# Left-side sums of an FFN computed once, kept in DRAM and fetched back; second part's down with four pairs by seven products

## The chip, the cores and the metric

One core of one Trainium2 chip. The time is device microseconds of one launch, the median of the runs given; lower is better. The core's engines that matter here are TensorE (PE in the profile, with PEld for its weight loads), VectorE (DVE), ScalarE (ACT), GpSimd (POOL) and SyncE (SP), which issues DMAs. Each engine works through its own instructions in a fixed order and waits on semaphores for the others.

## The reference

One decoder block on 256 tokens of width 2048, in f32:

```python
h = h + 0.5 * swiglu(rms_norm(h), w_gu1, w_down1)
h = h + hybrid_mixer(rms_norm(h), w_in, ..., w_out)
h = h + 0.5 * swiglu(rms_norm(h), w_gu2, w_down2)
h = h + sigmoid(rms_norm(h) @ w_pg) * (p @ w_pp)
out = rms_norm(h)
```

`swiglu(x)` is `(silu(x @ gate) * (x @ up)) @ w_down` with an inner width of 5632. The change touches the two FFNs only.

## The kernel before, in words

**Products in f32.** Every f32 weight tile `raw` is split into a rounded part `whi` (cast on ACT, L74) and a rest `wlo` (subtraction on DVE, L75); the left operand is split in the same way (`nTh` and `nTl`, or `hTh` and `hTl` for down). A product is three matmuls of 512 columns: whi by hi, wlo by hi, whi by lo. A *plain pair* is one `raw` tile of 512 KB (two k tiles by 512 columns) and 12 matmuls: two k tiles, two halves of the tokens, three each. `raw` has four buffers and is loaded on SP's queue; `whi` and `wlo` have three each.

**Seven products for eight.** A part of each large product is done by a scheme of Strassen's kind. Blocks of weights come as four quarters `R` (loads on POOL's queue, L276, but on SP's for the first such group of an FFN). Seven sums of them are made one after another, partly in DMA (L311) and partly on DVE (L304), and each is split into `shi` (ACT, L295) and `slo` (DVE, L296), which have two buffers each. Each of the seven products (`product`, L334 to L336) takes 3 matmuls for each of `ns` pairs. After the third and the fourth, result banks are added to each other over a copy `part` (ACT, L341; DVE, L342). Four of the seven need sums on the left side: `halves` adds hi and lo into `S` (L452), makes four differences in place (L458), and splits the result into `Sh` (ACT, L460) and `Sl` (DVE, L461), for two pairs at a time.

**Groups.** The inner width comes in eleven blocks of 512, in three parts: blocks 0 to 2, 3 to 6 and 7 to 10. A part is a list of gate-up groups (`gu`, one for each block, banks g and u) and then two down groups (`dn`, banks d, two blocks of 512 output columns each). `plan` writes the order of the weights by hand: through the plain pairs of a group it spreads the seven products of the *following* group, one behind each plain pair from the second or third on, and the loads of the quarters for the group after that. The tile framework then schedules all instructions into one order for each engine, which the change can alter even where the source does not. Lanes of generators are advanced by one step behind each plain pair (`lanes.step()`): lane 0 carries `down_input` (gated result, transposed by way of DRAM, to `hTh` and `hTl`), lane 1 carries `halves`.

**Around the change.** `halves("gu")` is called at the start of an FFN and again in the second down group of parts one and two, three times in all with the same input, since `Sh` and `Sl` have one buffer that down's sums also use. `halves("dn")` is called in the last gate-up group of each part. `NS_DOWN` was (2, 3, 3). For a third single pair `halves` yields once more, takes `S` from tag "nat" (four buffers) instead of "sil" (one), and keeps the sum in program order. `down_input` of a part's last block yields `last` times ahead of its last step: 3 for parts of four blocks, else 2.

Of the kernel before, what the change touches and what calls it, by code (L numbers as in the profile page):

```python
# [26 lines left out]
PARTS = ((0, 3), (3, 7), (7, 11))  # L27


NS = 4  # L30
NS_DOWN = tuple(3 if i1 - i0 == 4 else 2 for i0, i1 in PARTS)


W_IN_ORDER = (2, 0, 4, 3, 1, 5, 8, 10, 12, 9, 11, 13, 6, 7)
# [9 lines left out]
def block_kernel(ctx, tc, a, out):  # L44
    nc = tc.nc
# [14 lines left out]
    lanes = Lanes(4)  # L60
    dr = ctx.enter_context(tc.tile_pool(name="dr", bufs=1, space=bass.MemoryType.DRAM))
# [181 lines left out]
    current, sides = [None], {}  # L243
# [107 lines left out]
    def plan(n):  # L351
# [8 lines left out]
        groups = []  # L360
        for p, (i0, i1) in enumerate(PARTS):
            for i in range(i0, i1):
                plain = PLAIN[n]
                if i < plain:
                    src = [([a[f"w_gu{n}0"][2 * i + b][g] for g in range(KD // 2)], None) for b in range(2)]
                else:
                    src = [sources("w_gu" + n, 2 * (i - plain) + b) for b in range(2)]
                groups.append(Group("gu", p, [x[0] for x in src], [x[1] for x in src], NS if i >= plain else 0,
                                    len(groups) % 2))
            for nb in (0, 2):  # L370
                src = [sources(f"w_down{n}{p}", nb + b) for b in range(2)]
                groups.append(Group("dn", p, [x[0] for x in src], [x[1] for x in src], NS_DOWN[p], len(groups) % 2, nb))
        if n == "2":
            src = [sources("w_behind", b) for b in range(2)]
            groups.append(Group("behind", len(PARTS), [x[0] for x in src], [x[1] for x in src], NS_BEHIND,
# [41 lines left out]
    order += [("pair", a["w_pg"][2][g]) for g in range(KD // 2)] + [("pair", a["w_pp"][2])]  # L417
    order.append(("pair", a["w_pp"][3]))

    def halves(kind, his, los, ns, wait=0):  # L420


        for _ in range(wait):
            yield
        fp = current[0]

        sh = fp.tile([P, NS, 2, 2, P], F32R, tag="Sh", name="Sh")
        sl = fp.tile([P, NS, 2, 2, P], F32R, tag="Sl", name="Sl")

        def side(i, g):  # L430
            if i in (0, 4, 6):
                k, t = 2 * (g % 2) + (i > 0), i // 6
                c = slice(t * P, (t + 1) * P)
                return his[g // 2][:, k, c], los[g // 2][:, k, c]
            j, t = {1: (1, 1), 2: (0, 0), 3: (0, 1), 5: (1, 0)}[i]
            return sh[:, g, j, t, :], sl[:, g, j, t, :]

        sides[kind] = side

        for g0 in range(0, ns, 2):  # L440
            n = min(2, ns - g0)
            hi, lo = his[g0 // 2], los[g0 // 2]
            keep = lambda ins: ins
            if g0 and n == 1:

                keep = tc.keep_in_program_order
                yield
            if n == 2:
                x = fp.tile([P, 2 * NB], F32, tag="sil", name="S")
            else:  # L450
                x = act.tile([P, NB], F32, tag="nat", name="S", bufs=4)
            keep(nc.vector.tensor_tensor(out=x, in0=hi[:, 0:2 * n].bitcast(F32).rearrange("p k x -> p (k x)"),  # L452
                                         in1=lo[:, 0:2 * n].bitcast(F32).rearrange("p k x -> p (k x)"), op=ALU.add))
            xv = x.rearrange("p (g j t y) -> p g j t y", g=n, j=2, t=2)
            a11, a12, a21, a22 = (xv[:, :, j, t, :] for t in range(2) for j in range(2))
            for o, y, z, op in ((a22, a21, a22, ALU.subtract), (a21, a21, a11, ALU.subtract),
                                (a11, a22, a11, ALU.subtract), (a12, a11, a12, ALU.add)):
                nc.vector.tensor_tensor(out=o, in0=y, in1=z, op=op)  # L458
            sx = [y[:, g0:g0 + n].rearrange("p g j t y -> p (g j t y)") for y in (sh, sl)]
            nc.scalar.copy(sx[0], x)  # L460
            nc.vector.tensor_tensor(out=sx[1], in0=x, in1=sx[0], op=ALU.subtract)  # L461
            yield

    def ffn(n, nT, r, scale, next_norm, stat):
        xs = picker(*nT)
        late = callable(r)
        with tc.tile_pool(name="ffn", bufs=1) as fp:
            hTh, hTl = [], []
# [38 lines left out]

            nxt = None
            current[0] = fp
            lanes.add(1, halves("gu", *nT, NS, 6 if late else 0))  # L510
            for group, todo in ffn_plan[n]:
                if group.kind == "behind":
                    break
                dn = group.kind == "dn"
                i0 = PARTS[group.part][0]

                if dn and group.nb and not group.last:
                    lanes.add(1, halves("gu", *nT, NS))
# [8 lines left out]
                for kind, one in todo:  # L527
# [3 lines left out]
                    b, g = one  # L531
# [30 lines left out]
                    else:  # L562
# [7 lines left out]
                        hTl.append(tl)  # L570
                        i0, i1 = PARTS[group.part]

                        last = (3 if i1 - i0 == 4 else 2) if len(hTh) == i1 else 0
                        gen = down_input(outs, sil, th, tl, last)
                        next(gen)

# [801 lines left out]
```

## Time and profile before

| | |
|---|---|
| runs | 1946.30, 1947.38, 1947.69 us; median 1947.38 |
| profiled execution, span | 1944.1 us |
| runs' median less the span | 3.3 us |
| TensorE busy | 1927.9 us (99%), 8882 instructions |
| DVE, ACT, POOL busy | 82%, 60%, 8% |
| DMA | 475 MB, 244 GB/s over the span |

The first FFN takes the first 690 us of the span or so, the mixer stands up to about 1150, the second FFN up to about 1845. In a row of the timeline the first number is the start, the second the duration; a bracket at the end gives the engine's idle time before it and what ended it. Matmuls are pipelined: their listed 0.39 us overlap, and the distance between starts is what one costs. In a row of groups the numbers behind the bar are busy time, mean nanoseconds of one, and idle time before them with what ended it. In a row of windows the columns are length, busy time (and count) of PE, PEld, DVE, ACT, POOL, the granted clock, the DMA share and GB/s. In a row of waits they are total, times and the longest.

### The profile page before, as it was taken

The page shows a single profiled execution, that of the slowest core. Times are in us where ns is not written, and L with a number is a line of the kernel's source. Part 1 is how long each engine was busy: PE and PEld are TensorE (multiplying, and loading weights), DVE is VectorE, ACT ScalarE, POOL GpSimd, SP SyncE. Part 2 cuts the span into 40 slices and gives each one's busy share as a digit, 9 for nine tenths or more (in the row PEclk, how much of TensorE's full clock was granted, in tenths as well). Part 3 has the DMA queues.
Part 4 walks back from the last instruction along what each step waited for, and adds up shares of the span by engine and source line. Part 5 has one row for each costly group of instructions (what it writes and reads, how often), then busy time and mean ns, then how long its engine had stood idle before and what let it go on. Part 6 is the DMA issues. An engine that isn't in the chain of part 4 may idle for free.

```text
span 1944.1 us, 24295 instructions
## 1 busy us (share of the span) xinstructions
PE 1927.9 (99%) x8882; PEld 1593.1 (82%) x8882; DVE 1603.2 (82%) x1743; ACT 1163.4 (60%) x1358; POOL 148.8 (8%) x226
## 2 busy tenths in 40 slices
PE   9999999999999999999999999999999999999998
PEld 7888888888888888878788888888888888888887
DVE  7879988998889866797856679899888998889965
ACT  6655656566665567654555456566565755657654
POOL 0010110000001000010100000011000100001000
PEclk9999999999999999999999999999999999999999
DMA  8778898898898765556464776788898988989864
GB/s 306 269 217 291 256 292 272 248 296 247 269 288 255 224 218 171 173 167 218 159 215 157 243 278 229 236 268 285 260 278 253 306 257 261 264 263 273 253 212 147
DMA packets 144183, 475.06 MB, mean 244 GB/s; under 512 B 19648, under 2 KB 47296, under 8 KB 129856
## 3 DMA queue, kind: packets, MB, share of 16 engines
q1 hardware_dynamic: 104896, 293.78, 43.6%
q0 software_dynamic: 25920, 160.44, 29.9%
q10 hardware_dynamic: 13248, 19.30, 3.3%
q8 instruction: 69, 1.13, 0.2%
q14 instruction: 50, 0.41, 0.1%
HBM read 451.44 MB, written 22.02 MB: 244 GB/s over the span
## 4 chain that ended last, share of the span: by engine, by line
PE 91%; DVE 6%; issue 1%; DMA 1%; ACT 1%; POOL 0%; SPq 0%; POOLq 0%; DVEq 0%; ACTq 0%
PE d L540 5%; PE d L541 5%; PE d L542 5%; PE u L541 5%; PE u L542 5%; PE u L540 5%; PE g L541 4%; PE g L542 4%; PE pj L109 4%; PE pj L110 4%; PE pj L111 4%; PE g L540 4%; PE g L335 4%; PE g L334 4%; PE g L336 4%; PE u L334 3%
## 5 line engine op out<-in xcount | busy, mean ns | idle before, releaser
L74 ACT CAST whi<-raw 128x1024 fp32r<-128x1024 f32 (+1 forms) x489 | 511.7, 1050 | 420.0 <-PE pj L111 108.9
L75 DVE TENSOR_TENSOR wlo<-raw,whi 128x1024 fp32r<-128x1024 f32 (+1 forms) x489 | 590.8, 1217 | 155.8 <-ACT whi L74 153.1
L296 DVE TENSOR_TENSOR slo<-R,shi 128x2048 fp32r<-128x2048 f32 (+2 forms) x224 | 444.4, 1987 | 99.9 <-ACT shi L295 99.7
L295 ACT CAST shi<-R 128x2048 fp32r<-128x2048 f32 (+2 forms) x224 | 374.0, 1673 | 185.6 <-DVE R L304 74.4
L109 PE MATMUL pj<-whi,nTh 128*128 128x512 f32 x448 | 179.4, 401 | 0.0
L110 PE MATMUL pj<-wlo,nTh 128*128 128x512 f32 x448 | 175.3, 391 | 1.4 <-DVE wlo L75 1.4
L111 PE MATMUL pj<-whi,nTl 128*128 128x512 f32 x448 | 174.9, 390 | 0.0
L541 PE MATMUL d<-wlo,hTh 128*128 128x512 f32 x448 | 174.4, 389 | 0.0
L542 PE MATMUL d<-whi,hTl 128*128 128x512 f32 x448 | 174.0, 389 | 0.0
L540 PE MATMUL d<-whi,hTh 128*128 128x512 f32 x448 | 173.1, 390 | 0.0
L541 PE MATMUL g<-wlo,nTh 128*128 128x512 f32 x400 | 156.1, 390 | 0.6 <-DVE wlo L75 0.6
L540 PE MATMUL g<-whi,nTh 128*128 128x512 f32 x400 | 154.9, 390 | 1.2 <-ACT whi L74 0.9
L542 PE MATMUL g<-whi,nTl 128*128 128x512 f32 x400 | 155.9, 390 | 0.0
L541 PE MATMUL u<-wlo,nTh 128*128 128x512 f32 x400 | 155.7, 389 | 0.1
L542 PE MATMUL u<-whi,nTl 128*128 128x512 f32 x400 | 155.6, 389 | 0.0
L540 PE MATMUL u<-whi,nTh 128*128 128x512 f32 x400 | 154.2, 389 | 0.0
L304 DVE TENSOR_TENSOR R<-R 128x2048 f32<-128x2048 f32 (+2 forms) x68 | 135.4, 1991 | 0.1
L110 PEld LDWEIGHTS pj<-wlo,nTh 128*128 128x128 f32 x448 | 84.2, 188 | 19.2 <-DVE wlo L75 3.0
L540 PEld LDWEIGHTS d<-whi,hTh 128*128 128x128 f32 x448 | 84.1, 188 | 17.9 <-ACT hTh L499 0.7
L542 PEld LDWEIGHTS d<-whi,hTl 128*128 128x128 f32 x448 | 84.1, 188 | 17.7
L111 PEld LDWEIGHTS pj<-whi,nTl 128*128 128x128 f32 x448 | 84.1, 188 | 17.5
L541 PEld LDWEIGHTS d<-wlo,hTh 128*128 128x128 f32 x448 | 84.1, 188 | 17.4
(327 smaller groups left out, 3482.5 us busy)
## 6 DMA issues: line engine op xcount, KB each, us to landing
raw<-in_w_gu SPq DMA_DIRECT2D x199, 512.0 KB, 5.7
raw<-in_w_down SPq DMA_DIRECT2D x112, 512.0 KB, 6.4
raw<-in_w_in SPq DMA_DIRECT2D x112, 512.0 KB, 3.4
R<-in_w_gu2q POOLq DMA_DIRECT2D x54, 1024.0 KB, 8.1
R<-in_w_gu1q POOLq DMA_DIRECT2D x48, 1024.0 KB, 8.7
raw<-in_w_out SPq DMA_DIRECT2D x32, 512.0 KB, 4.4
R<-in_w_down11q POOLq DMA_DIRECT2D x12, 768.0 KB, 6.8
R<-in_w_down12q POOLq DMA_DIRECT2D x12, 768.0 KB, 6.3
```

What stands on the lines that cost most here:

```text
L74: nc.scalar.copy(hi[:, j, :], raw[:, j, :])
L75: nc.vector.tensor_tensor(out=lo[:, j, :], in0=raw[:, j, :], in1=hi[:, j, :], op=ALU.subtract)
L109: nc.tensor.matmul(outs[t], xh[:, c], whi[:, j, :], start=st, stop=False)
L110: nc.tensor.matmul(outs[t], xh[:, c], wlo[:, j, :], start=False, stop=False)
L111: nc.tensor.matmul(outs[t], xl[:, c], whi[:, j, :], start=False, stop=sp)
L295: keep(nc.scalar.copy(hi, w))
L296: nc.vector.tensor_tensor(out=lo, in0=w, in1=hi, op=ALU.subtract)
L304: keep(nc.vector.tensor_tensor(out=self.raw[x], in0=self.raw[x], in1=self.raw[y], op=ALU.add))
L334: nc.tensor.matmul(out, xh, whi[:, g, :], start=st, stop=False, skip_group_check=True)
L540: nc.tensor.matmul(out, xh[:, c], whi[:, j, :], start=st, stop=False, skip_group_check=True)
L541: nc.tensor.matmul(out, xh[:, c], wlo[:, j, :], start=False, stop=False, skip_group_check=True)
L542: nc.tensor.matmul(out, xl[:, c], whi[:, j, :], start=False, stop=sp, skip_group_check=True)
```

## The change

`NS_DOWN` becomes (2, 4, 3): each of the second part's two down groups has seven products of twelve matmuls instead of nine, and eight plain pairs instead of ten; its quarters, `shi` and `slo` are 2048 columns wide instead of 1536. Since it has four pairs, its `halves("dn")` now makes two sums of full size, without the extra yield and the kept order. `last` for that part goes from 3 to 2.

The gate-up sums are made once for each FFN. Four lane steps after they are done, `Sh` and `Sl` are written to a DRAM tile `sides` (two writes of 1 MB each on SP's queue), and in the second down group of parts one and two `kept_sides` fetches them (8 loads of 256 KB each on SP's queue) where `halves("gu")` was called before. `Sh` and `Sl` have another layout, so that each of the four sums is contiguous over the pairs.

```diff
-NS_DOWN = tuple(3 if i1 - i0 == 4 else 2 for i0, i1 in PARTS)
+NS_DOWN = (2, 4, 3)
...
-    def halves(kind, his, los, ns, wait=0):
-
-
-        for _ in range(wait):
-            yield
-        fp = current[0]
-
-        sh = fp.tile([P, NS, 2, 2, P], F32R, tag="Sh", name="Sh")
-        sl = fp.tile([P, NS, 2, 2, P], F32R, tag="Sl", name="Sl")
+    def new_sides(kind, his, los):
+
+        sh, sl = [current[0].tile([P, 4, NS, P], F32R, tag=x, name=x) for x in ("Sh", "Sl")]
 
         def side(i, g):
             if i in (0, 4, 6):
                 k, t = 2 * (g % 2) + (i > 0), i // 6
                 c = slice(t * P, (t + 1) * P)
                 return his[g // 2][:, k, c], los[g // 2][:, k, c]
-            j, t = {1: (1, 1), 2: (0, 0), 3: (0, 1), 5: (1, 0)}[i]
-            return sh[:, g, j, t, :], sl[:, g, j, t, :]
+            jt = {1: 3, 2: 0, 3: 1, 5: 2}[i]
+            return sh[:, jt, g, :], sl[:, jt, g, :]
 
         sides[kind] = side
+        return sh, sl
+
+    def kept_sides(his, los, copy):
+
+        yield
+        both = new_sides("gu", his, los)
+        for jt in (3, 0, 1, 2):
+            for i in range(2):
+                nc.sync.dma_start(out=both[i][:, jt].bitcast(F32), in_=copy[:, i, jt])
+
+    def halves(kind, his, los, ns, wait=0, copy=None):
+
+
+        for _ in range(wait):
+            yield
+        fp = current[0]
+
+        both = new_sides(kind, his, los)
...
-            sx = [y[:, g0:g0 + n].rearrange("p g j t y -> p (g j t y)") for y in (sh, sl)]
-            nc.scalar.copy(sx[0], x)
-            nc.vector.tensor_tensor(out=sx[1], in0=x, in1=sx[0], op=ALU.subtract)
-            yield
+            xs = x.rearrange("p (g c y) -> p c g y", g=n, c=4)
+            sx = [y[:, :, g0:g0 + n, :] for y in both]
+            nc.scalar.copy(sx[0], xs)
+            nc.vector.tensor_tensor(out=sx[1], in0=xs, in1=sx[0], op=ALU.subtract)
+            yield
+        if copy is not None:
+            for _ in range(4):
+                yield
+            for i in range(2):
+                nc.sync.dma_start(out=copy[:, i], in_=both[i].bitcast(F32))
...
-            lanes.add(1, halves("gu", *nT, NS, 6 if late else 0))
+            copy = dr.tile([P, 2, 4, NS, P], F32, tag="sides", name="sides", bufs=2)
+            lanes.add(1, halves("gu", *nT, NS, 6 if late else 0, copy))
...
                 if dn and group.nb and not group.last:
-                    lanes.add(1, halves("gu", *nT, NS))
+                    lanes.add(1, kept_sides(*nT, copy))
...
-                        last = (3 if i1 - i0 == 4 else 2) if len(hTh) == i1 else 0
+                        last = (4 - NS_DOWN[group.part] + 2 if i1 - i0 == 4 else 2) if len(hTh) == i1 else 0
```

How the change moves instructions at the three places that the prediction speaks of (line numbers behind the changed functions are larger by 13 to 20).

**First place: ACT at the start of the first FFN**, from the last statistics of the norm (`junk,stat`) over the first gated results (`sil`) to the first split of a quarter sum (`shi`). Before:

```order
L222 ACTIVATE junk,stat<-h 128x512
L74 CAST whi<-raw 128x1024 x3
L505 ACT_TABLE_LOAD
L505 ACTIVATE sil<-g_121,rstd_515 128x512
L74 CAST whi<-raw 128x1024
L505 ACTIVATE sil<-g_122,rstd_515 128x512
L74 CAST whi<-raw 128x1024
L295 CAST shi<-R 128x2048
```

Now:

```order
L222 ACTIVATE junk,stat<-h 128x512
L74 CAST whi<-raw 128x1024
L524 ACT_TABLE_LOAD
L524 ACTIVATE sil<-g_122,rstd_518 128x512
L524 ACTIVATE sil<-g_123,rstd_518 128x512
L74 CAST whi<-raw 128x1024 x5
L506 DMA scr_578<-tb 128x1024
L295 CAST shi<-R 128x2048 x2
```

Two of the three weight casts ahead of the table load, and the one between the two activations, now stand behind both activations.

**Second place: DVE in the last gate-up group of the second part (first FFN)**, from the sum `S` for down's left sides to the end of the second `Sl`. Before:

```order
L458 TENSOR_TENSOR S<-S 128x2x128
L452 TENSOR_TENSOR S<-hTh,hTl 128x512
L458 TENSOR_TENSOR S<-S 128x2x128
L458 TENSOR_TENSOR S<-S 128x128
L75 TENSOR_TENSOR wlo<-raw,whi 128x1024
L458 TENSOR_TENSOR S<-S 128x128
L461 TENSOR_TENSOR Sl<-S,Sh 128x1024
L458 TENSOR_TENSOR S<-S 128x128
L296 TENSOR_TENSOR slo<-R,shi 128x1536
L458 TENSOR_TENSOR S<-S 128x128
L461 TENSOR_TENSOR Sl<-S,Sh 128x512
L75 TENSOR_TENSOR wlo<-raw,whi 128x1024
```

Now:

```order
L296 TENSOR_TENSOR slo<-R,shi 128x2048
L475 TENSOR_TENSOR Sl<-S,Sh 128x4x256
L465 TENSOR_TENSOR S<-hTh,hTl 128x1024
L471 TENSOR_TENSOR S<-S 128x2x128
L75 TENSOR_TENSOR wlo<-raw,whi 128x1024
L471 TENSOR_TENSOR S<-S 128x2x128
L75 TENSOR_TENSOR wlo<-raw,whi 128x1024
L471 TENSOR_TENSOR S<-S 128x2x128
L75 TENSOR_TENSOR wlo<-raw,whi 128x1024
L471 TENSOR_TENSOR S<-S 128x2x128
L75 TENSOR_TENSOR wlo<-raw,whi 128x1024
L475 TENSOR_TENSOR Sl<-S,Sh 128x4x256
```

The second sum now starts behind the first `Sl` and the third `slo` instead of ahead of both, and four weight subtractions stand between it and its `Sl`.

**Third place: TensorE a little later**, where the second product of the following down group ends and the next (bank `d_2816` before, `d_2811` now) begins. Before:

```order
L540 MATMUL u_2474<-whi,nTh 128x512
L541 MATMUL u_2474<-wlo,nTh 128x512
L334 MATMUL d_2816<-shi,Sh 128x512
L542 MATMUL u_2474<-whi,nTl 128x512
L540 MATMUL u_2475<-whi,nTh 128x512
L541 MATMUL u_2475<-wlo,nTh 128x512
L542 MATMUL u_2475<-whi,nTl 128x512
L540 MATMUL u_2474<-whi,nTh 128x512
L541 MATMUL u_2474<-wlo,nTh 128x512
L542 MATMUL u_2474<-whi,nTl 128x512
L335 MATMUL d_2816<-slo,Sh 128x512
L336 MATMUL d_2816<-shi,Sl 128x512
```

Now:

```order
L336 MATMUL d_2809<-shi,Sl 128x512
L334 MATMUL d_2809<-shi,Sh 128x512
L335 MATMUL d_2809<-slo,Sh 128x512
L336 MATMUL d_2809<-shi,Sl 128x512
L334 MATMUL d_2811<-shi,Sh 128x512
L334 MATMUL d_2808<-shi,hTh 128x512
L335 MATMUL d_2811<-slo,Sh 128x512
L336 MATMUL d_2811<-shi,Sl 128x512
L334 MATMUL d_2811<-shi,Sh 128x512
```

Plain u matmuls stood between the first row of that product and its `slo` rows; now one row of the product after it (`d_2808`, first row) stands there, and no plain ones.

More of the change, by code (lines that the diff above doesn't have):

```diff
@@ L371, in plan @@
                 src = [sources(f"w_down{n}{p}", nb + b) for b in range(2)]
-                groups.append(Group("dn", p, [x[0] for x in src], [x[1] for x in src], NS_DOWN[p], len(groups) % 2, nb))
+                groups.append(Group("dn", p, [x[0] for x in src], [x[1] for x in src], NS_DOWN[p],
+                                    len(groups) % 2, nb))
         if n == "2":
```

## The prediction

> **What bounds the kernel now.** I read the page first, then what TensorE waits for, then the timeline at the places where the change alters the order.
>
> ```profile
> span 1944.1 us, 24295 instructions
> PE 1927.9 (99%) x8882; PEld 1593.1 (82%) x8882; DVE 1603.2 (82%) x1743; ACT 1163.4 (60%) x1358; POOL 148.8 (8%) x226
> PEclk9999999999999999999999999999999999999999
> PE 91%; DVE 6%; issue 1%; DMA 1%; ACT 1%; POOL 0%; SPq 0%; POOLq 0%; DVEq 0%; ACTq 0%
> ```
>
> TensorE is busy 99% of the span at an undiminished clock, and the chain that ended last runs through it for 91%. DVE at 82% has room on the average. The table of TensorE's waits, whose top rows follow, adds up to a few microseconds:
>
> ```profile
> PE pj L110 <- DVE wlo L75: 1.4, 3, 0.6
> PE vp L1109 <- DVE R L1130: 1.2, 1, 1.2
> PE idle L130 <- DVE stat L229: 1.1, 1, 1.1
> ```
>
> So two things can move the time: fewer matmuls, which pays in full, and new places where TensorE runs dry, which cost in full. Relief of DVE or ACT pays nothing by itself. Each engine works through its own rows in a fixed order, so a row that is moved ahead of another on ACT or DVE can starve TensorE even where the engine has idle time on the average.
>
> **The change, part by part.**
>
> *Matmuls.* These are rows of TensorE, ACT and DVE at the first FFN's start; the price of one matmul is the distance between starts.
>
> ```profile
> 48.31 0.39 PE L542 MATMUL g<-whi,nTl 128*128 128x512 f32 x1
> 48.53 0.39 PE L540 MATMUL u<-whi,nTh 128*128 128x512 f32 x1
> 48.76 0.39 PE L541 MATMUL u<-wlo,nTh 128*128 128x512 f32 x1
> ```
>
> From 48.31 to 48.76 are two steps, 0.225 us each (0.2267 over longer stretches). The second part's down has two groups in each FFN. Each had seven products of nine matmuls (63) and ten plain pairs of twelve (120), 183 in all; now it has seven of twelve (84) and eight plain pairs (96), 180. That is 3 fewer in each of 4 groups: 12 x 0.2267 = **-2.7 us**.
>
> *The first FFN's start.* Each activation of the first gate's result (`sil`) needs a finished PSUM bank and, once, a table load.
>
> ```profile
> 46.01 1.05 ACT L74 CAST whi<-raw 128x1024 fp32r<-128x1024 f32 x1 [1.67 <-PE u L542]
> 48.10 1.28 ACT L505 ACT_TABLE_LOAD   x1 [1.03 <-PE g L542]
> 49.39 0.69 ACT L505 ACTIVATE sil<-g,rstd 128x512 f32<-128x512 f32 x1
> 49.98 1.04 ACT L74 CAST whi<-raw 128x1024 fp32r<-128x1024 f32 x1
> 50.92 0.69 ACT L505 ACTIVATE sil<-g,rstd 128x512 f32<-128x512 f32 x1
> ```
>
> ```profile
> 47.10 1.23 DVE L75 TENSOR_TENSOR wlo<-raw,whi 128x1024 fp32r<-128x1024 f32 x1 [1.50 <-ACT whi L74]
> 51.05 1.23 DVE L75 TENSOR_TENSOR wlo<-raw,whi 128x1024 fp32r<-128x1024 f32 x1 [2.72 <-ACT whi L74]
> ```
>
> The cast at 46.01 and its subtraction at 47.10 feed the u matmuls that start at 48.53. In the changed order on ACT (first place shown above) only one cast of these three stands ahead of the table load; the cast for those u matmuls comes behind the load and both activations. The load cannot move: it waits for the last g matmuls. So load 48.10, first activation 49.39, second 49.98 to 50.67, cast 50.6 to 51.65, subtraction 51.65 to 52.9. TensorE finishes g at 48.53 and waits until 51.65, 3.1 us; it has two matmuls that need only the cast (0.45), and then waits for the subtraction until 52.9, another 0.8. After that the casts are ahead again. **+3.9 us.** From below it is 0 if the cast were not in fact behind the activations; from above 3.9 + 1.2, if one more subtraction came too late. I take 3.9, since every step has its own row. [...]
>
> *The second part's down products.* DVE and TensorE around the last gate-up group of that part in the first FFN:
>
> ```profile
> 342.78 1.75 DVE L296 TENSOR_TENSOR slo<-R,shi 128x1536 fp32r<-128x1536 f32 x1
> 344.45 0.70 DVE L482 STREAM_TRANSPOSE tb<-sil 128x512 f32<-128x512 f32 x1
> 345.08 1.72 DVE L304 TENSOR_TENSOR R<-R 128x1536 f32<-128x1536 f32 x1
> ...
> 347.34 1.18 DVE L75 TENSOR_TENSOR wlo<-raw,whi 128x1024 fp32r<-128x1024 f32 x1
> 348.45 1.21 DVE L452 TENSOR_TENSOR S<-hTh,hTl 128x1024 f32<-128x1024 f32 x1
> 349.58 1.75 DVE L296 TENSOR_TENSOR slo<-R,shi 128x1536 fp32r<-128x1536 f32 x1
> ...
> 353.25 0.42 DVE L458 TENSOR_TENSOR S<-S 128x256 f32<-128x256 f32 x1
> 353.58 1.22 DVE L75 TENSOR_TENSOR wlo<-raw,whi 128x1024 fp32r<-128x1024 f32 x1
> ...
> 355.06 0.69 DVE L452 TENSOR_TENSOR S<-hTh,hTl 128x512 f32<-128x512 f32 x1
> ...
> 357.53 1.22 DVE L461 TENSOR_TENSOR Sl<-S,Sh 128x1024 fp32r<-128x1024 f32 x1
> ...
> 361.51 0.69 DVE L461 TENSOR_TENSOR Sl<-S,Sh 128x512 fp32r<-128x512 f32 x1 [0.69 <-ACT Sh L460]
> ```
>
> ```profile
> 350.46 0.39 PE L334 MATMUL d<-shi,hTh 128*128 128x512 f32 x1
> ```
>
> ```profile
> L296 DVE TENSOR_TENSOR slo<-R,shi 128x2048 fp32r<-128x2048 f32 x133 | 304.1, 2288 | 81.0 <-ACT shi L295 80.8
> L304 DVE TENSOR_TENSOR R<-R 128x2048 f32<-128x2048 f32 x42 | 95.6, 2277 | 0.1
> L295 ACT CAST shi<-R 128x2048 fp32r<-128x2048 f32 x133 | 254.5, 1916 | 139.3 <-DVE R L304 55.2 <-PE u L336 34.7 <-PE g L336 21.1
> L341 ACT COPY part<-d 128x512 f32<-128x512 f32 x48 | 27.8, 584 | 2.7 <-PE d L336 2.6
> 345.00:360.00 15.00, 15.00 (x68) 12.40 (x67) 15.00 (x19) 7.77 (x7) 0.89 (x1) 1.00 0.84 223
> ```
>
> Now the second pair's sum S had its own buffer and began at 355.06, ahead of the first Sl at 357.53, and the second Sl was done by 362.1, with many u matmuls still to come. In the changed order (second place) the second S shares one buffer with the first, so it stands behind the first Sl, and four weight subtractions stand between it and the second Sl. DVE has no pause here (15.00 of 15), so its rows can be added by their distances in the rows above: tb 0.63, wlo 1.12, S 1.13, each difference 0.33 to 0.34, Sl 1.14 (its mean of 1.22 less 0.08), and for 2048 columns slo 2.21 and R 2.20 (again means less the 0.08 by which neighbours overlap). From the first product's slo to the second Sl stand 2 tb, 2 R, 7 wlo, 2 S, 8 differences, 2 slo, 2 Sl: 1.3 + 4.4 + 7.8 + 2.3 + 2.7 + 4.4 + 2.3 = 25.2. The start is 344.45 + 0.54 (the first slo is longer too), so the second Sl is done at **370.2**.
>
> TensorE starts the first product at 350.46 and has 88 matmuls before it needs that Sl: 12 of the product, 12 g, 48 u, 16 of the second and third product. 350.46 + 88 x 0.2267 = 370.4, plus 0.65 on the way (the tenth row of that list, a u subtraction, ends at 357.0 where TensorE arrives at 356.35): 371.1. It does not wait for Sl itself, but by then it has no u matmul left. Both weight buffers of the products (`shi` has two) are held until the second product ends at 372.0. Behind that, in line: cast of the fourth product's `shi` (1.92) to 373.9, where TensorE has been idle since 372.9 (1.0); the sum of a result on DVE (to 373.7), its copy on ACT (0.58), and the next `shi` (1.92) to 376.4, for which one matmul stands in front of the fourth product's `slo` rows (third place); `slo` is done at 376.5. That is a second wait of 2.2. The sixth product's `shi` comes 0.5 late in the same way. 0.65 + 1.0 + 2.2 + 0.5 = **4.4 us**. The second FFN has the same rows 1143 us later:
>
> ```profile
> 1504.51 0.69 DVE L461 TENSOR_TENSOR Sl<-S,Sh 128x512 fp32r<-128x512 f32 x1 [0.69 <-ACT Sh L460]
> ```
>
> so **+8.8** for both. From below: nothing, if TensorE had matmuls left when the buffers came free (that needs DVE 4 us earlier); from above, if DVE comes 1.5 us later than I add up, 5.9 each. I keep the sum, nearer the middle.
>
> *A small gain.* Left sums at the third part's first product leave DVE; the uneven steps there vanish (0.35 for 0.23, two in each FFN): **-0.5**.
>
> ```profile
> 444.24 0.39 PE L542 MATMUL d<-whi,hTl 128*128 128x512 f32 x1
> 444.59 0.50 PE L334 MATMUL u<-shi,Sh 128*128 128x512 f32 x1
> ```
>
> *What I cost at nothing.* DVE loses 33 us of sums (8.2 in each of four places) and 8 wlo, and gains 28 slo and 8 R at 0.54 more each; it bounds nothing on the average. The writes and reads of the sides (12 MB) and 6 MB more of quarters against 4 MB less of plain weights go over queues with room:
>
> ```profile
> 24.00:34.00 10.00, 10.00 (x45) 8.28 (x45) 9.93 (x16) 8.76 (x17) 0.00 (x0) 1.00 1.03 399
> raw<-in_w_gu SPq DMA_DIRECT2D x199, 512.0 KB, 5.7
> ```
>
> One set of sides is 2 MB, 5.3 us at the 399 GB/s that this stretch moved. The fetch is issued about 20 us before its first use. Queued behind it on SP are plain weights, which have four buffers: 4 x 12 x 0.2267 = 10.9 us of matmuls, less 5.7 for landing, leaves 5.2 of cover.
>
> **Sum** against the profiled execution: 1944.1 - 2.7 + 3.9 + 8.8 - 0.5 = 1953.6 of span. The median of the runs (1947.4) lies 3.3 above the span, so **1956.9 us**.
>
> **Rivals.**
> 1. *SP's queue holds the weights up* (slower still). In each FFN one write and two fetches of 2 MB stand ahead of weight loads. For it: 5.3 against a cover of 5.2, and less cover where the quarters fill the engines as well. Against it: the cast at 46.01 waits for TensorE's buffers, not for a DMA. If each of these six let TensorE dry for 0.8, the sum is 1956.9 + 4.8 = 1961.7. [...]
> 2. *DVE arrives early* (no change). If the 33 us taken from DVE let it run 4 us ahead into the second part's last group, the second place costs nothing: 1956.9 - 8.8 = 1948.1. Against it: ahead of that group DVE was not behind; it idled 2.0 us in 15, waiting for buffers, so there is little lead to win.
>
> ```profile
> 330.00:345.00 15.00, 15.00 (x67) 12.41 (x67) 12.98 (x12) 7.51 (x8) 1.08 (x2) 1.00 0.80 283
> ```
>
> 3. *Neither wait shows* (not slower, the other side). The casts at the start would have to be done before the load, and DVE early; the matmuls alone are left: 1947.4 - 2.7 - 0.5 = 1944.2. It decides if ACT's cast precedes the load by any means; the order of the rows speaks against it.
>
> **How the numbers follow.** The forecast has 0.62, rival 1 0.15, rival 2 0.14, rival 3 0.09. No change means within 0.2%, 3.9 us, about what a measurement of this kernel can tell. Slower: 0.62 + 0.15 = 0.77, plus 0.01 from rival 2's upper end; same: 0.13 of rival 2 and 0.05 of rival 3, 0.18; faster: 0.04. The forecast's own range is 1953 to 1961 (part two's place between 2.4 and 5.9 each); for 8 in 10 it reaches down to rival 2 and up to rival 1: 1948 to 1963.
>
> **What would show it.** The profile after should have TensorE waiting some 4 us near 49 us for a cast, two waits of 1 to 2.5 us near 375 and again near 1520, the second Sl of that part done near 370 + 4, 12 matmuls fewer, and no wait for `raw` behind the sides. I am wrong if TensorE's waits stay at a few microseconds in total, or if the large ones name a DMA.

## The result, and the profile after

The changed kernel takes **1968.16 us** (median of 4 runs, 1967.11 to 1968.64) against 1946.84 for the kernel before (median of 4, 1945.95 to 1947.69): a ratio of **1.0109**, 95% interval 1.0096 to 1.0122. It is slower by 21 us, where 10 were forecast, and above the range.

The page of the changed kernel, span, engines and chain:

```profile
span 1966.5 us, 24213 instructions
PE 1934.6 (98%) x8870; PEld 1595.8 (81%) x8870; DVE 1591.5 (81%) x1687; ACT 1161.8 (59%) x1342; POOL 148.9 (8%) x226
...
PE 86%; DVE 5%; DMA 2%; ACT 2%; issue 1%; POOL 0%; SPq 0%; ACTq 0%; POOLq 0%; DVEq 0%
```

There are twelve matmuls fewer (8870 for 8882), and yet TensorE's busy time grew by 6.7 us: a first sign that matmuls themselves became slower somewhere. TensorE's waits in the changed kernel (total, times, longest):

```profile
PE d L334 <- ACT shi L295: 6.8, 5, 1.8
PE d L335 <- DVE slo L296: 4.4, 4, 1.5
PE u L560 <- ACT whi L74: 2.9, 1, 2.9
PE u L561 <- DVE wlo L75: 1.6, 3, 0.7
```

The first row belongs to the second part, the third to the start of the first FFN, and most of the fourth to the second part. These are the waits that were forecast, but for 1.1 us of the first row, which stand later in the second FFN. The second row was not: 2.6 of its 4.4 us stand in the first part's down (1.1 and 1.5), the rest late in the second part. What follows the waits is in the windows of the changed kernel around the start (first three rows) and around the second part of the first FFN (next three) and of the second FFN (last two); the granted clock is the third number from the right:

```profile
44.00:48.00 4.00, 4.00 (x20) 3.30 (x19) 0.00 (x0) 0.03 (x1) 0.00 (x0) 1.00 0.72 291
48.00:53.00 5.00, 2.02 (x6) 0.87 (x5) 1.51 (x2) 4.99 (x6) 0.00 (x0) 0.81 0.00 0
53.00:57.60 4.60, 4.60 (x11) 3.58 (x12) 2.22 (x3) 0.51 (x2) 0.00 (x0) 0.50 0.85 299
...
376.00:380.00 4.00, 4.00 (x18) 3.01 (x17) 3.08 (x4) 3.56 (x7) 0.00 (x0) 1.00 1.02 415
380.00:384.00 4.00, 1.19 (x4) 0.40 (x3) 3.97 (x5) 4.00 (x4) 0.00 (x0) 1.00 0.23 90
385.50:388.50 3.00, 3.00 (x8) 2.32 (x8) 2.12 (x2) 0.18 (x1) 0.56 (x1) 0.51 0.75 289
...
1555.80:1559.60 3.80, 1.60 (x6) 0.67 (x4) 2.69 (x3) 3.39 (x4) 0.00 (x0) 1.00 0.99 224
1559.60:1563.00 3.40, 3.38 (x8) 2.71 (x9) 3.40 (x3) 0.54 (x1) 0.00 (x0) 0.52 0.81 287
```

The same stretch of the kernel before:

```profile
53.00:57.60 4.60, 4.60 (x22) 3.79 (x21) 4.60 (x5) 2.30 (x2) 0.00 (x0) 1.00 1.01 422
```

Behind each of these three waits the clock granted to TensorE is 0.50 to 0.52, for 6.8 us at the start and 3.4 us at the other two: 11 matmuls in 4.6 us where there were 22. The wait of the last two rows is not the one that was forecast for the second FFN. That one, 1530 to 1534 us, has the same rows as 380 to 384 in the first FFN, and behind it the clock stays at 1.00:

```profile
1530.00:1534.00 4.00, 1.13 (x4) 0.37 (x3) 3.98 (x5) 4.00 (x4) 0.00 (x0) 1.00 0.21 83
1534.00:1536.40 2.40, 2.40 (x11) 2.00 (x11) 2.40 (x2) 0.68 (x1) 0.56 (x1) 1.00 0.34 55
```

In the timeline of the changed kernel the starts of the slow matmuls are 0.43 us apart instead of 0.227:

```profile
53.79 0.63 PE L561 MATMUL u<-wlo,nTh 128*128 128x512 f32 x1
54.22 0.63 PE L562 MATMUL u<-whi,nTl 128*128 128x512 f32 x1
54.65 0.63 PE L560 MATMUL u<-whi,nTh 128*128 128x512 f32 x1
```

Where the 22.4 us of span went, from the distances between starts of matmuls beyond 0.227 us, summed over each place in both traces:

| place | forecast | measured | of it at half the clock |
|---|---|---|---|
| first FFN's start, 40 to 60 us | +3.9 | +6.5 | 2.5 |
| behind it, 60 to 80 us | 0 | +0.6 | |
| first part's down, both FFNs | 0 | +1.0 | |
| second part, first FFN | +4.4 | +7.6 | 1.6 |
| second part, second FFN | +4.4 | +9.6 | 1.6 |
| second FFN's start | 0 | +0.7 | |
| third part's start, both FFNs | -0.5 | -0.7 | |
| twelve matmuls | -2.7 | -2.7 | |
| sum | +9.5 | +22.6 | 5.7 |

### The profile page after: what moved, and what is told of

Its sections match the earlier page's. It is cut to its first block, busy times and chain, and to the rows that moved or that the text cites. A ratio compares the mean times of both kernels' runs of the same rounds, so it can differ in the third digit from the quotient of the medians.

```text
span 1966.5 us, 24213 instructions
## 1 busy us (share of the span) xinstructions
PE 1934.6 (98%) x8870; PEld 1595.8 (81%) x8870; DVE 1591.5 (81%) x1687; ACT 1161.8 (59%) x1342; POOL 148.9 (8%) x226
## 4 chain that ended last, share of the span: by engine, by line
PE 86%; DVE 5%; DMA 2%; ACT 2%; issue 1%; POOL 0%; SPq 0%; ACTq 0%; POOLq 0%; DVEq 0%
PE d L562 5%; PE d L561 4%; PE d L560 4%; PE u L561 4%; PE u L562 4%; PE u L560 4%; PE pj L109 4%; PE pj L110 4%; PE pj L111 4%; PE g L561 4%; PE g L562 4%; PE g L560 4%; PE g L335 4%; PE g L336 4%; PE g L334 4%; PE u L336 3%
## 5 line engine op out<-in xcount | busy, mean ns | idle before, releaser
L74 ACT CAST whi<-raw 128x1024 fp32r<-128x1024 f32 (+1 forms) x481 | 503.2, 1050 | 429.6 <-PE pj L111 107.3
L75 DVE TENSOR_TENSOR wlo<-raw,whi 128x1024 fp32r<-128x1024 f32 (+1 forms) x481 | 581.5, 1217 | 167.9 <-ACT whi L74 167.0
L296 DVE TENSOR_TENSOR slo<-R,shi 128x2048 fp32r<-128x2048 f32 (+2 forms) x224 | 459.2, 2055 | 117.4 <-ACT shi L295 116.7
L295 ACT CAST shi<-R 128x2048 fp32r<-128x2048 f32 (+2 forms) x224 | 385.8, 1726 | 190.6 <-DVE R L304 72.5
L561 PE MATMUL d<-wlo,hTh 128*128 128x512 f32 x416 | 161.9, 389 | 0.0
L560 PE MATMUL d<-whi,hTh 128*128 128x512 f32 x416 | 161.1, 389 | 0.0
L562 PE MATMUL d<-whi,hTl 128*128 128x512 f32 x416 | 160.9, 389 | 0.0
L109 PEld LDWEIGHTS pj<-whi,nTh 128*128 128x128 f32 x448 | 84.2, 188 | 16.6
L335 PE MATMUL u<-slo,Sh 128*128 128x512 f32 x234 | 91.2, 390 | 1.1 <-DVE slo L296 1.1
L561 PEld LDWEIGHTS u<-wlo,nTh 128*128 128x128 f32 x400 | 75.6, 189 | 19.8 <-DVE wlo L75 4.2
```

Source lines behind the costliest of these rows:

```text
L74: nc.scalar.copy(hi[:, j, :], raw[:, j, :])
L75: nc.vector.tensor_tensor(out=lo[:, j, :], in0=raw[:, j, :], in1=hi[:, j, :], op=ALU.subtract)
L109: nc.tensor.matmul(outs[t], xh[:, c], whi[:, j, :], start=st, stop=False)
L295: keep(nc.scalar.copy(hi, w))
L296: nc.vector.tensor_tensor(out=lo, in0=w, in1=hi, op=ALU.subtract)
L335: nc.tensor.matmul(out, xh, wlo[:, g, :], start=False, stop=False, skip_group_check=True)
```

## The experiments

The theory (A): each wait comes from the order of rows on ACT and DVE as worked out ahead, and a long wait is followed by matmuls at half the clock. Its rivals: the sides' transfers cause the waits (B, C), the slow matmuls have another cause (D). For the second part: the shared buffer of S (F) or the wider rows on DVE (G).

**One half of the change alone: down.** Kernel before with

```diff
-NS_DOWN = tuple(3 if i1 - i0 == 4 else 2 for i0, i1 in PARTS)
+NS_DOWN = (2, 4, 3)
...
-                        last = (3 if i1 - i0 == 4 else 2) if len(hTh) == i1 else 0
+                        last = (4 - NS_DOWN[group.part] + 2 if i1 - i0 == 4 else 2) if len(hTh) == i1 else 0
```

> The kernel before with the second part's down at four pairs by seven products and its last = 2 alone; sums made three times, nothing in DRAM. Theory A (the new waits of the second part come from DVE's order in its last gate-up group, and the granted clock halves behind them): the 7.6 us (first FFN) and 9.6 us (second) that TensorE lost there with the whole change stay, less 2.7 for twelve matmuls: about 1947 + 14.5 = 1961, and ACT's order at the start is as before, with no wait near 49 us. Rival B (the sides' transfers hold up what the second part needs): without them those waits go, and the time is 1944 to 1948.

Measured 1958.62 us against 1946.52 (ratio 1.0061, 1.0046 to 1.0076): +12.1, where theory A had some 14.5. The waits and the slow matmuls of the second part are there without any transfer of sides, which rejects B. Windows of that kernel:

```profile
373.00:377.00 4.00, 1.31 (x5) 0.52 (x3) 3.97 (x5) 4.00 (x3) 0.00 (x0) 1.00 0.23 95
378.00:381.50 3.50, 3.50 (x10) 2.71 (x9) 2.73 (x2) 0.06 (x1) 0.76 (x2) 0.51 0.67 243
```

**The other half alone: sides.** Changed kernel with

```diff
-NS_DOWN = (2, 4, 3)
+NS_DOWN = (2, 3, 3)
```

> The changed kernel with the second part's down at three pairs again; the sums are made once and fetched. Theory A: only the start of the first FFN (6.5 us of lost matmul time, of them 2.6 at half the granted clock), 0.6 near 70 us, some 1 us at the first part's down, 0.7 at the second FFN's start, and 0.7 won at the third part: about 1947 + 8 = 1955; no wait over 1 us between 345 and 410 us. Rival B (the fetched sides hold up SP's queue): waits at the second part as well, 1960 or more.

Measured 1952.75 us (1.0033, 1.0021 to 1.0044): +6.2, where theory A had 8. The second part shows no wait, and the start's wait is the same 2.9 on `whi`. The halves add up to 18.3 of 21.3; by the distances in the traces the other 3 are in the second part, 2.2 in the second FFN and 0.7 in the first, below.

**The writes on another queue.** Changed kernel with

```diff
-                nc.sync.dma_start(out=copy[:, i], in_=both[i].bitcast(F32))
+                nc.gpsimd.dma_start(out=copy[:, i], in_=both[i].bitcast(F32))
```

> The changed kernel with the two writes of the sides issued on POOL's queue instead of SP's; all else is the same. ACT then has its three casts ahead of the table load again, as in the kernel before. Theory A (the order of the casts makes the wait): the start's 6.5 us go, and the second FFN's 0.7: about 1968 - 7 = 1961. Rival C (the wait comes from the transfer itself, 2 MB beside the weights): it stays, 1966 to 1968.

ACT's three casts stand ahead of the table load again. Measured 1959.20 us (1.0065, 1.0050 to 1.0080): 9 less than the changed kernel, where 7 were expected, and no loss at all between 40 and 60 us. Most of the other 2 is the late wait of the second FFN (1556 to 1560 us), which is down to 0.3 us here. The same bytes are written; so the order of the casts made the wait, and C is rejected. The changed kernel's own trace agrees: three tiles `raw` landed at 44.51, 45.73 and 46.97, while ACT stood idle for 6.47 us up to the table load at 47.97, with their casts behind it:

```profile
47.97 1.28 ACT L524 ACT_TABLE_LOAD   x1 [6.47 <-PE g L562]
```

The loads do land later behind the sides (44.51 where the kernel before has 39.99), but that alone let TensorE run dry nowhere. Why the scheduler orders ACT differently for another queue stays open.

**Matmuls in the wait.** Changed kernel, and in a later run the sides-only kernel, with

```diff
                     elif b == 0:
+                        if late and n == "1":
+                            idle = mx_ps("idle")
+                            for i in range(13):
+                                tc.keep_in_program_order(nc.tensor.matmul(idle, nT[0][i % 4][:, 0, 0:P], ...))
```

> The changed kernel with 13 matmuls of 512 columns on normalised activations added on TensorE between the first gate's last matmul and the u matmuls that wait; nobody reads their result. They take 2.95 us of a wait of 3.1 us. Theory A (the granted clock halves because TensorE stood still): the clock stays at 1.0 and the matmuls behind the wait start 0.227 us apart instead of 0.43, 2.6 us less: about 1965.5. Rival D (the matmuls behind the wait are slow because weights or banks come late): they stay 0.43 apart and the time is 1968 to 1969.

> The sides-only kernel with 13 idle matmuls (results unread) on TensorE in the wait at the start of the first FFN; that wait is the only one over 2 us in the program. Theory A (the clock halves because TensorE stood still): no matmuls 0.43 us apart behind it, 1952.75 - 2.4 = 1950.3, and the runs close together. Rival D (the matmuls are slow for another reason, or the clock falls anyway): 1952.5 to 1953.5.

On the changed kernel: 1969.33 us (1.0122, 1.0105 to 1.0139), its runs from 1962.83 to 1972.41; the profiled one is the lowest, with a mean clock of 0.997 where the others list 0.995. In its trace the slow matmuls at the start are gone, as A says, but the median did not fall. The spread hid the answer, so the sides-only kernel, with one wait, was taken: 1952.16 us (1.0027, 1.0016 to 1.0038), 0.6 less than without the filling instead of 2.4. Windows of the sides-only kernel without the filling:

```profile
48.00:51.40 3.40, 0.45 (x3) 0.13 (x1) 0.15 (x1) 3.39 (x5) 0.00 (x0) 0.91 0.06 23
51.40:53.00 1.60, 1.56 (x3) 0.84 (x4) 1.60 (x2) 1.60 (x2) 0.00 (x0) 0.50 0.00 0
53.00:57.00 4.00, 4.00 (x11) 3.07 (x11) 1.62 (x3) 0.12 (x1) 0.00 (x0) 0.50 0.85 324
```

With it:

```profile
48.00:51.40 3.40, 3.09 (x13) 2.01 (x11) 0.81 (x1) 3.39 (x6) 0.00 (x0) 1.00 0.00 0
51.40:53.00 1.60, 1.14 (x5) 0.97 (x6) 1.60 (x3) 1.04 (x2) 0.00 (x0) 1.00 0.14 28
53.00:57.00 4.00, 4.00 (x20) 3.29 (x19) 3.71 (x5) 1.06 (x1) 0.00 (x0) 1.00 1.01 378
...
68.00:72.00 4.00, 1.40 (x6) 0.83 (x5) 3.57 (x3) 2.40 (x3) 0.00 (x0) 0.91 0.88 362
72.00:76.00 4.00, 4.00 (x14) 3.18 (x13) 4.00 (x4) 1.32 (x2) 0.00 (x0) 0.66 0.75 241
```

With TensorE kept at work the clock stays at 1.00, and 20 matmuls run where 11 did: D is rejected for this place. But TensorE then arrives earlier at the next late sum, near 68 us, stands there for 2.8 us instead of 1.3, and there the clock falls (0.66 over 72 to 76 us). The wait was handed on, and the gain with it.

**Shared buffer or wide rows.** Kernel before, third pair's S in the shared buffer:

```diff
             if g0 and n == 1:
-                keep = tc.keep_in_program_order
-                yield
+                pass
...
-                x = act.tile([P, NB], F32, tag="nat", name="S", bufs=4)
+                x = fp.tile([P, 2 * NB], F32, tag="sil", name="S")[:, 0:NB]
```

> The kernel before, with three pairs, but the third pair's sum S takes the one buffer of the first two pairs' S, without the extra yield and the kept order: the shared buffer of the change without its wider rows. Theory F (the shared buffer, which puts the second S behind the first Sl, makes the second part's wait): 5 us in each FFN as in the down-only kernel, 1956 to 1958. Theory G (the wider slo, R and second S, more work for DVE than TensorE's matmuls cover there, make most of it): 1 to 2 us in each FFN, 1948.5 to 1950.5.

And the down-only kernel with narrow rests:

```diff
-                nc.vector.tensor_tensor(out=lo, in0=w, in1=hi, op=ALU.subtract)
+                m = 3 if self.kind == "dn" and self.ns == 4 else self.ns
+                nc.vector.tensor_tensor(out=lo[:, 0:m], in0=w[:, 0:m], in1=hi[:, 0:m], op=ALU.subtract)
...
-                nc.tensor.matmul(out, xh, wlo[:, g, :], start=False, stop=False, skip_group_check=True)
+                m = min(g, 2) if self.kind == "dn" else g
+                nc.tensor.matmul(out, xh, wlo[:, m, :], start=False, stop=False, skip_group_check=True)
...
```

> The down-only kernel, but for the second part's down DVE makes slo and the sums R for the first 1536 of 2048 columns alone; the fourth pair's matmuls use the third pair's slo in place of their own. The rests of the fourth pair and DVE's share of its sums are left out; matmuls, ACT, DMAs and the shared S stay. DVE has 9.7 us less in each FFN (18 rows at 0.54). Theory G (DVE's load): waits of the second part under 1 us in each FFN, the twelve matmuls show: 1944 to 1946. Theory F (shared S, or ACT's longer shi): 3 to 5 us in each FFN stay, 1952 to 1957.

The shared buffer alone: 1950.45 us (1.0020, 1.0011 to 1.0029), 1.9 us in each FFN. But this kernel has three pairs in the third part too, so the shared buffer stands at two places of each FFN: by distances it costs 1.2 us in the second part and 1.1 in the third, and the change brings only the first. The narrow rests: 1946.04 us (0.9996, 0.9987 to 1.0005), 12.6 less than the down-only kernel, with the shared buffer and ACT's longer casts still there. So F is rejected: the shared buffer alone and the longer casts don't make the wait, and it takes the wider rows on DVE. Their length is only a part of it, though. The second Sl begins here at 364.02,

```profile
364.02 1.23 DVE L464 TENSOR_TENSOR Sl<-S,Sh 128x1024 fp32r<-128x1024 f32 x1
```

6.4 us earlier than in the down-only kernel. Five rows narrower by 0.54 make 2.7 of that; most of the rest comes from the order, which the scheduler changed as well: one weight subtraction instead of four stands between the second S and its Sl. No run separates the two. The twelve matmuls fewer don't show in the time, since waits of 0.7 and 1.0 us remain a little later. Windows of the down-only kernel and, behind it, of the narrow one, for 345 to 360 us:

```profile
345.00:360.00 15.00, 14.31 (x63) 11.54 (x62) 14.88 (x15) 8.16 (x7) 0.89 (x1) 1.00 0.78 205
```

```profile
345.00:360.00 15.00, 15.00 (x68) 12.43 (x67) 14.96 (x16) 9.38 (x8) 1.77 (x2) 1.00 0.83 221
```

DVE is full in both (14.88 and 14.96 of 15.00 us); with narrower rows it gets through 16 instructions instead of 15, and TensorE through 68 matmuls instead of 63.

**Sides without either wait.** Sides-only kernel with the writes on POOL's queue:

> Sums made once and fetched, their writes on POOL's queue, the second part's down at three pairs as before: the one half of the change without either wait. Theory A: the start as before, 1 us lost at the first part's down in both FFNs, 0.7 won at the third part's start: 1946.5 to 1947.5, no difference. If relief of 25 us for DVE were worth anything by itself: 1944 or less.

Measured 1946.16 us (0.9997, 0.9989 to 1.0006): no difference. The fetches on SP's queue cost nothing that shows, though each piece of 256 KB takes 8.0 us to land; and 27.5 us of work taken from DVE (busy for 1575.7 us instead of 1603.2) bring nothing. This row of the changed kernel's DMA issues belongs to it:

```profile
Sh<-sides SPq DMA_DIRECT2D x16, 256.0 KB, 8.0
```

**DVE's work spread.** The whole change with POOL's writes and

```diff
+                if group.ns and group.kind == "gu" and follower.kind == "dn" and follower.ns == 4:
+                    first = 3
...
-        for g0 in range(0, ns, 2):
-            n = min(2, ns - g0)
+        four = kind == "dn" and ns == 4
+        for g0, n in (((0, 2), (2, 1), (3, 1)) if four else [(g0, min(2, ns - g0)) for g0 in range(0, ns, 2)]):
...
```

> The whole change (four pairs by seven, sums made once), with the sides written on POOL's queue, the seven products of the second part's first down group begun behind the fourth plain pair instead of the third, and its second S made as two sums of 512 columns in the four-buffer tag, both in one lane step. It is meant to give DVE's wider rows time in the following group. Theory G (DVE's load in one stretch, bunched): the second part costs 1 to 2 us in each FFN, about 1947 - 2.7 + 1 (first part's down) + 3 = 1948, against 1959.2 with the writes on POOL alone. Theory F (the wide rows cost wherever they stand): 1956 or more.

Measured 1963.45 us (1.0090, 1.0076 to 1.0103): worse than with the writes on POOL alone, and in the range given for F, but not for its reason. In the trace the waits that it was meant for are down to some 1.4 us in each FFN, with the wide rows still there and S in buffers of its own; but one of 5 us stands behind them. ACT there (the bracket is its idle time and what ended it), and the windows:

```profile
404.07 1.14 ACT L521 CAST hTh<-tT 128x512 fp32r<-128x512 f32 x2 [6.50 <-DMA tT<-scr]
405.11 3.69 ACT L295 CAST shi<-R 128x2048 fp32r<-128x2048 f32 x2
```

```profile
397.00:401.50 4.50, 4.50 (x21) 3.75 (x20) 3.01 (x2) 0.56 (x1) 0.00 (x0) 1.00 0.97 196
401.50:407.00 5.50, 0.41 (x2) 0.00 (x0) 1.29 (x2) 2.93 (x4) 0.00 (x0) 1.00 1.05 361
407.00:410.00 3.00, 2.94 (x7) 2.36 (x8) 2.96 (x2) 2.75 (x3) 0.07 (x1) 0.50 0.30 120
```

The transposed h of the part's last block comes through DRAM; its cast `hTh` stands on ACT ahead of the casts `shi`, and TensorE waits for those while ACT waits for the transfer. The changed kernel has the same wait, smaller: 1.05 us on ACT in the first FFN, and in the second

```profile
1554.82 0.62 ACT L518 CAST hTh<-tT 128x512 fp32r<-128x512 f32 x1 [2.98 <-DMA tT<-scr]
1555.35 1.90 ACT L295 CAST shi<-R 128x2048 fp32r<-128x2048 f32 x1
```

This makes the 3 us that the two halves lack: by distances 0.9 and 2.7 us of waiting in the two FFNs and 1.7 of slow matmuls behind the second, less 0.8 of this wait and 1.5 of slow matmuls that the down-only kernel has in the second FFN. With eight plain pairs instead of ten, the pairs that need the last block begin two pairs earlier. That is not the whole cause: the down-only kernel and the one with the writes on POOL have the same eight pairs and the same `last`, and there ACT waits 0 and 0.73, and 1.53 and 0.56 us for that cast in the two FFNs. In the second FFN of the changed kernel the h is written to DRAM at 1539.98 and read back from 1544.48 on, 4.5 us later, where the first FFN and the down-only kernel have 2.7; why is not known. A version with `last` at 3 as before was not tried. How much of the lateness is the wider quarters on the DMA engines, which are busy all the time there (0.97 and 1.05 of the share), stays open.

**A pause for TensorE alone.** Kernel before with two matmuls of 128 columns and fillings of their operand on POOL between them (8, 13 and 20):

```diff
+                rest = act.tile([P, NB], F32, tag="junk", name="rest", bufs=1)
+                tc.keep_in_program_order(nc.gpsimd.memset(rest, 0.0))
+                tc.keep_in_program_order(nc.tensor.matmul(out[:, 0:P], rest[:, 0:P], rest[:, 0:P], start=True, stop=True))
+                for _ in range(8):
+                    tc.keep_in_program_order(nc.gpsimd.memset(rest, 0.0))
+                tc.keep_in_program_order(nc.tensor.matmul(out[:, 0:P], rest[:, 0:P], rest[:, 0:P], start=True, stop=True))
```

> The kernel before with one pause made for TensorE alone in the third part's down of the first FFN: a matmul of 128 columns, 8 fillings of its operand on POOL (0.52 us each by the row of such a filling, 4.1 us), then a second such matmul ten matmuls later (2.3 us): 1.9 us of standing still. Results unread. Theory A (a long stand halves the clock, a short one doesn't): the pause alone, 1946.6 + 1.9 = 1948.5, no matmuls 0.43 apart. Rival D (the clock has no part in it): the same 1948.5.

> As the kernel with the short pause, with 13 fillings: 6.7 - 2.3 = 4.4 us of standing still. Theory A: matmuls 0.43 us apart for some 5 us behind it, 4.4 + 2.5: 1953.5, and the granted clock 0.5 in the rows there. Rival D: 1946.6 + 4.4 = 1951.

> As the two kernels with a pause, with 20 fillings on POOL. In the one with 13 the first matmul ran 6 us ahead of the second and TensorE stood still for 0.6 us only; 7 more at 0.53 us make 4.3 us of standing still, alone in the program. Theory A (standing still halves the granted clock): 4.3 + 2 to 2.8 us, 1952.6 to 1953.4, the matmuls behind it 0.43 us apart for some 5 us. Rival D: the pause alone, 1950.6, matmuls 0.23 apart.

1946.01 (0.9999), 1947.16 (1.0002) and 1947.69 us (1.0008, 0.9999 to 1.0017). These failed as experiments: the scheduler put up to 11 us of other matmuls between the two, and TensorE stood still for 0.2, 0.6 and 0.8 us. They say nothing on the clock.

**All stands of TensorE in the 14 traces.** In place of the failed pauses, each stand of more than 1.2 us in total (steps of more than 0.6 us beyond the usual distance; those less than 4 us apart are one stand) and the matmuls some 0.43 us apart in the 7 us behind it:

| stand | how many | with 5 to 10 slow matmuls behind | with 0 or 1 |
|---|---|---|---|
| 1.2 to 2.3 us | 40 | 0 | 40 |
| 2.55 and 2.8 us | 2 | 2 | 0 |
| 3.1 us (the first FFN's start) | 2 | 2 | 0 |
| 3.3 us (the second part, 1.24 + 2.05) | 8 | 6 | 2 |
| 4.9 and 5.3 us | 2 | 2 | 0 |

The same stand of 3.3 us, in the same rows, is followed by 8, 8, 8, 7, 5, 5, 1 and 1 slow matmuls. The length of a stand doesn't decide by itself. What does can be read from where the clock changes. In each of the 14 traces all changes of the granted clock lie whole multiples of 3.413 us apart, and each stretch at 0.50 between matmuls lasts 3.41 us, at the start twice that. So here are windows of the changed kernel cut on this grid, around the start, the forecast stand in the first FFN, the same stand in the second FFN, and the late wait there (the first number behind the comma is TensorE's busy time):

```profile
47.65:51.06 3.41, 0.92 (x5) 0.41 (x3) 0.00 (x0) 3.08 (x4) 0.00 (x0) 1.00 0.01 2
51.06:54.47 3.41, 2.92 (x6) 1.92 (x7) 2.36 (x2) 2.29 (x3) 0.00 (x0) 0.50 0.23 47
...
382.15:385.57 3.42, 1.64 (x8) 1.26 (x8) 3.42 (x3) 2.78 (x3) 0.57 (x1) 1.00 0.02 5
385.57:388.98 3.41, 3.41 (x10) 2.67 (x9) 2.09 (x3) 0.66 (x2) 0.56 (x1) 0.50 0.82 310
...
1529.03:1532.45 3.42, 1.89 (x8) 0.99 (x6) 3.40 (x5) 3.42 (x4) 0.00 (x0) 1.00 0.54 216
1532.45:1535.86 3.41, 2.08 (x9) 1.76 (x10) 3.41 (x3) 2.23 (x2) 0.56 (x1) 1.00 0.14 17
1535.86:1539.27 3.41, 3.40 (x16) 2.46 (x15) 3.31 (x5) 2.44 (x3) 0.55 (x1) 1.00 0.81 300
...
1556.34:1559.75 3.41, 1.34 (x5) 0.81 (x6) 2.48 (x2) 2.85 (x4) 0.00 (x0) 1.00 1.00 228
1559.75:1563.16 3.41, 3.41 (x9) 2.64 (x10) 3.41 (x3) 0.70 (x1) 0.00 (x0) 0.50 0.76 274
```

Where TensorE was idle for 1.78 us of a window or more, the next window runs at 0.50; in the second FFN the grid cuts the same stand into 1.53 and 1.34 us, and the clock stays. In all 14 traces, from 12 us on to TensorE's last matmuls, 12 windows at the full clock are followed by one at half of it, and they are idle for 1.78 to 3.41 us. Of all others the most idle has 1.78 too (behind the matmuls put into the wait, near 70 us), the next 1.65. So the border lies close to 1.78 of 3.41 us in this case. It was found afterwards and no run was made to test it, and why the start's low clock lasts two windows stays open. Since the grid lies elsewhere in each execution, the same kernel can pay at such a place in one and not in the next; that is a likely reason for the wide spread of some kernels here (9.6 us with matmuls in the wait), and is not shown.

## Why the prediction was wrong

**Right: where and why TensorE runs dry.** The start's wait was worked out as 3.1 us, then 0.8. The changed kernel shows 2.95 idle ahead of the u matmuls (3.1 beyond the usual distance) and two steps of 0.4 up to the first matmul that needs the subtraction, 3.9 in all. Of the 0.8 the trace lists only 0.04 as idle, since the two matmuls ahead of it already ran at half the clock and filled the time. Its rows on ACT are those of the list: table load at 47.97, both activations from 49.26, casts from 50.42. In the second part the fourth product's cast was to hold TensorE for 1.0 and the next for 2.2; measured 1.07 and 1.78 idle, 1.23 and 2.05 by distances (the 0.5 at the sixth product does not show in the changed kernel; 0.4 in the down-only one):

```profile
381.76 0.50 PE L334 MATMUL d<-shi,Sh 128*128 128x512 f32 x1 [1.07 <-ACT shi L295]
384.04 0.50 PE L334 MATMUL d<-shi,hTh 128*128 128x512 f32 x1 [1.78 <-ACT shi L295]
```

The second Sl was put at 370.2 for its end. The down-only kernel, which has no delay at its start, shows it from 370.43 to 371.65, 1.4 later; the u subtraction held TensorE for 0.84 instead of 0.65. One link is not as it was written: ahead of the fourth product's cast ACT has the activations of the gated result (`sil`), which wait for the second Sl, and it goes from them to the cast without a pause. So the rows don't tell whether these or the buffers of the second product set its time.

```profile
370.43 1.22 DVE L461 TENSOR_TENSOR Sl<-S,Sh 128x1024 fp32r<-128x1024 f32 x1
```

The matmul term (-2.7) and the small gain (-0.7 for -0.5) hold too.

**The step that failed: new places where TensorE runs dry "cost in full", and no more than that.** The sum priced each wait at its length and kept 0.2267 us for the matmuls behind it, from a trace in which the granted clock stayed at 1.00 from 4.3 us to behind the last matmul, and no wait was longer than 1.4 us. In the runs, 12 stands that left TensorE idle for 1.78 us or more of one window of 3.41 were paid with a second price: in the changed kernel some 1.6 us of matmuls at half the clock at either second part, and 2.5 at the start, where two windows were slow. That is 5.7 of the 13 us that the sum was short of. The filling shows it as a cause: with matmuls in the wait at the start the slow ones behind it go (clock 1.00 instead of 0.50, 20 matmuls in 4.00 us instead of 11). Three things of it stand in the traces: the distance of 0.426 to 0.427 us between starts, the clock of 0.50, and the fixed grid of 3.413 us. Why an idle window has this effect is not shown. A forecast with waits of 3 us, twice the longest in the trace of before, should have had a price for the matmuls behind them as a rival.

**The second step: what is late next.** The prediction followed the line of casts to the sixth product and stopped. It did not follow the gated result of the last block, which shares the buffer of S and is late with it (its activation ran at 358.85 and 361.39 before, at 371.68 in the down-only kernel), goes through DRAM, and holds ACT and the casts `shi` behind it: 0.9 us in the first FFN and 2.7 in the second, by distances. The down-only kernel has the same late result and lost 0 and 0.8 us by it, so how much this path costs was not to be had from the order alone.

**Small terms at nothing** were +0.6 (behind the start), +1.0 (first part's down, for a reason that stays open) and +0.7 (second FFN's start). They come with the sides, as the sides-only kernel shows all three as well.

**The rivals.** Weights held up on SP's queue (rival 1) did not let TensorE run dry: the loads behind the writes landed 4.5 us later, but no wait of TensorE names `raw`, and with the writes on POOL the fetched sides cost nothing (0.9997). DVE did not arrive early (rival 2), and both waits showed (rival 3).

## What to carry to other kernels

Where TensorE is busy 99% of the time, ask of each new wait how much of one window of 3.41 us it can leave idle. In these traces windows with up to 1.65 us idle cost the wait alone; of those with 1.78 or more all but one were followed by matmuls some 0.43 us apart, which cost another 1.5 to 2.5 us where they were summed up. From that an estimate: a stand of less than 1.8 us is safe wherever the grid lies, one of more than 3.6 (twice 1.78) cannot be, and one between is fragile, since a change elsewhere shifts it on the grid. Work taken off an engine that is not the bound was worth nothing here (27.5 us of DVE's, ratio 0.9997), but work added to it in one stretch cost much (12.6 us between the down-only kernel and the narrow one, the changed order included); compare the busy time of both engines group by group. And before a transfer goes into a queue that the scheduler plans with, look at where the rows of the *other* engines land: the same two writes cost 9 us on one queue and nothing that shows on another.

## What was not expected of the hardware

TensorE's granted clock fell to 0.50 for 3.41 us (at the start 6.83) in 12 places, each behind a window of a fixed grid of 3.413 us in which TensorE had been idle for 1.78 us or more; one other window with 1.78 and all with less were not followed by it. A stand of 3.3 us that the grid cut in two did not lower it, and none of 40 stands of up to 2.3 us did. A chain through DRAM of 512 KB, written and read back in four pieces, took from 386.59 (issue of the write) over 393.04 (issue of the first read) to 404.07 (first use, for which ACT waited 6.50) in the kernel with spread work, 17.5 us; in the kernel before it was 12.7, from 382.86 to a first use at 395.54 without a wait, in the same place.
